# A hybrid mLSTM and gMLP layer: the first weight chunk multiplied pass by pass, and each mLSTM head's operands loaded beside the head before

## The chip, the cores and the metric

The kernel runs on one core of one Trainium2 chip. The metric is the device time of one execution in microseconds (us). The kernel before was run three times: 1581.03, 1575.95 and 1568.94 us, median 1575.95. One further execution was recorded by the hardware profiler.

## What is computed

The layer takes x (512 tokens of 2048 features, float32), and returns the same shape. Cut to what matters:

```python
xn = rmsnorm(x, norm_w)
q, k, v_m, o_m, z_m, i_pre, f_pre, u_g, v_g, z_g = split_cols(xn @ w_in)
q, k = silu(causal_depthwise_conv([q, k]))          # width 4
log_i, log_f = i_pre + b_i, log_sigmoid(f_pre + b_f)
# 8 mLSTM heads (q, k: 128 wide, v: 256), causal, chunks of 128 tokens:
#   S = (q @ k.T) * P,  P = exp of gate sums, row by row stabilised
#   h = (S @ v + state part) / max(|denominator|, exp(-m))
y_m = rmsnorm_per_head(h) * mlstm_norm_w * sigmoid(o_m) * silu(z_m)
# 8 gMLP groups: token mixing by a lower triangular 128 x 128 matrix
y_g = gelu(u_g) * (w_s @ layernorm(gelu(v_g)) + b_s) * silu(z_g)
out = rmsnorm(x + [y_m, y_g] @ w_out, final_norm_w)
```

## The kernel before, in words

Every float32 operand of a matmul is cut into a high and a low half of a shorter format (a cast on ScalarE, ACT; a subtraction on VectorE, DVE), and a product is the sum of three matmuls: high x high, high x low, low x high. So each operand costs a cast and a subtraction before TensorE (PE) can use it. Names end in h and l accordingly: xah and xal, wh and wl, qkh and qkl. In the first chunk the high and low halves of one quarter of x both carry the name a.

The program is written with a framework of tiles: pools with a few buffers each, and semaphores where one engine's instruction needs another's result. It decides the final order on each engine from the order in the code and from priorities, so the order is read from the compiled program. The stages are:

1. **The first unit** (lines 735 to 741). Eight chunks of weights, each 128 x 1024 floats (w_first), are multiplied by eight chunks of x in the plain way: 24 matmuls of 128 x 512 per chunk and 8 small gate products (L271). For each chunk the loop calls `load_x` and `load` (DMA, some chunks ahead), `split_x` (L197: the scaling by the norm's weight L205, casts L206, L207 and L210, subtractions L208, L209 and L211), `split` (L168 and L169) and `sums_x` (L215, further sums for later units). Ahead of the loop stand `split_x(0)`, `split(0)`, `gate_weights()`, `split_x(1)` and `split(1)`. The loads of x and of the first weights come in two halves.
2. **Units 1 to 27** (`products`, L769): the seven products of a Strassen scheme on the other columns of w_in, 42 matmuls of 128 x 256 per chunk, with DMA-accumulated weight sums (L150, L151), and conv, gelu, silu and layer norm beside them.
3. **The output projection of the gMLP half** (L803 to L831): four column quarters dq times eight groups g, 24 matmuls `og` of 128 x 512 each. Beside it runs the mLSTM. Its steps are closures in a queue `bg`, of which `run_bg(6)` takes six behind each chunk; a `pause` is an empty step.
4. **The output projection of the mLSTM half** (`q_m`), then the last groups (`fo`), the residual and the final norm.

The queue of stage 3 holds, in this order: `gates` (L286: gate sums, scans and exponentials, whose result c goes to DRAM as c_dram), six pauses, `gate_shifts` (transposes tps of the rows go), four pauses, `gate_columns` (transposes tps of gb and gr, copied to gst). Then for each head h, by `queue_head`:

- `st_load`: GpSimd (POOL) issues the loads of q and k (tiles qr), ACT casts (L530), DVE subtracts (qkl, L531).
- `st_load_v` and `st_cb`: loads and splits of v (tiles vr, L542 and L543), and the load of the row c of this head to all partitions (cb, L548).
- four `st_s`: the score products s in PSUM (L556 to L558), the weights P from cb (L563 to L567), their product p (DVE, L569) and its split (sh, sl, L581 and L582).
- two `turn` steps of the head before: transposes ytm of oz (L462), copied and stored for stage 4.
- four `st_sv`: the products nv (L595 to L597), copied to h and den by ACT (L598, L599).
- `st_norm`: the load of oz (L605), the denominator da (L609), its reciprocal rr, four squares jk on ACT (L616), sq, rn on POOL (L620), hc.
- `st_out`: oz scaled by h and hc (L628).

s, nv, ytm and the gate transposes share four PSUM banks (pm), taken in turn; the `og` sums hold the other four. A bank of s comes free when p (L569) has read it, one of ytm or nv when ACT has copied it.

Of the kernel before, what the change touches and what calls it, by code (L numbers as in the profile page):

```python
# [9 lines left out]
F32 = mybir.dt.float32  # L10
# [37 lines left out]
def hybrid_layer(ctx, tc, xs, x, w_first, w_mid, w_gate, w_out, w_last, par, bif, ws_t, sgu, fin_w, out):  # L48
# [17 lines left out]
    def temp(name, dt=F32):  # L66
        return tp.tile([P, S], dt, tag="t", name=name)
# [84 lines left out]

    def split(n):
# [5 lines left out]
        if kind == "std":  # L159
            if n >= NF0 + 2:  # L160
                h = xb.tile([P, 2, S], F32R, tag="xb", name=f"fh{n}")
                l = xb.tile([P, 2, S], F32R, tag="xb", name=f"fl{n}")
            else:
                h, l = (wp.tile([P, WS], F32R, tag=tag, name=f"{tag}{n}", bufs=bufs)[
                    :, OFF:OFF + 1024].rearrange("p (a b) -> p a b", a=2) for tag, bufs in (("wh", 3), ("wl", 3)))
            f = t[:, 0:1024].rearrange("p (a b) -> p a b", a=2)
            for a in ((slice(0, 1), slice(1, 2)) if n == 0 else (slice(0, 2),)):
                nc.scalar.copy(h[:, a, :], f[:, a, :])  # L168
                nc.vector.tensor_tensor(l[:, a, :], f[:, a, :], h[:, a, :].bitcast(F32), op=ALU.subtract)  # L169
            splits[n] = (h, l)  # L170
            return
# [25 lines left out]
    def split_x(j):  # L197
        if j >= NP:
            return
        (ra, rb) = xr[j]  # L200
        ah, al = (xa.tile([P, 3, H], F32R, tag="xa", name=f"xa{c}{j}") for c in "hl")
        a21 = temp(f"a21_{j}", F32R).rearrange("p (a b) -> p a b", a=2)
        for b, r in enumerate((ra, rb)):
            k = j + NP * b
            nc.vector.tensor_scalar(r, r, prm[:, C_NW + k:C_NW + k + 1], None, op0=ALU.mult)  # L205
        nc.scalar.copy(ah[:, 0, :], ra[:, 1, :])  # L206
        nc.scalar.copy(a21[:, 0, :], ra[:, 0, :])  # L207
        nc.vector.tensor_tensor(al[:, 0, :], ra[:, 1, :], ah[:, 0, :].bitcast(F32), op=ALU.subtract)  # L208
        nc.vector.tensor_tensor(a21[:, 1, :], ra[:, 0, :], a21[:, 0, :].bitcast(F32), op=ALU.subtract)  # L209
        nc.scalar.copy(ah[:, 1:3, :], rb)  # L210
        nc.vector.tensor_tensor(al[:, 1:3, :], rb, ah[:, 1:3, :].bitcast(F32), op=ALU.subtract)  # L211
        X[j] = [(ah[:, s, :], al[:, s, :]) for s in range(3)]
        A21[j] = (a21[:, 0, :], a21[:, 1, :])
# [416 lines left out]

    def queue_head(h):
        if h < NH:
            bg.append(lambda: st_load(h))
            bg.append(lambda: st_load_v(h))
            bg.append(lambda: st_cb(h))
            for s0 in range(NT):
                bg.append(lambda s0=s0: st_s(h, s0))
        if h > 0:
            for f in range(2):
                w = prm[:, C_MW + 2 * (h - 1) + f:C_MW + 2 * (h - 1) + f + 1]  # L640
                bg.append(lambda f=f, w=w: turn("m", h - 1, f, oz_t[h - 1], w))
            bg.append(mark(("m", h - 1)))
        if h < NH:
            for t0 in range(NT):
                bg.append(lambda t0=t0: st_sv(h, t0))
            bg.append(lambda: st_norm(h))
            bg.append(lambda: st_out(h))
# [60 lines left out]
    split_x(0)  # L708
    split(0)
# [6 lines left out]
    for j in range(NP):  # L716
# [16 lines left out]
        for q in range(4):  # L733
            cs = slice((q % 2) * P, (q % 2 + 1) * P)
            for kk in range(2):
                xh, xl = blocks[kk][q // 2]
                st, sp_ = (j == 0 and kk == 0), (j == NP - 1 and kk == 1)
# [51 lines left out]
    bg.append(gates)  # L789
    bg.extend([pause] * 6)  # L790
    bg.append(gate_shifts)
    bg.extend([pause] * 4)
    bg.append(gate_columns)
    for h in range(NH + 1):
        queue_head(h)

# [193 lines left out]
```

## Time and profile before

| | |
|---|---|
| runs | 1581.03, 1575.95, 1568.94 us; median 1575.95 |
| profiled execution | 1567.65 us |
| its span in the profile | 1565.6 us |
| mean granted TensorE clock | 0.995 |
| PE / PEld / DVE / ACT / POOL busy | 1531.3 / 1465.1 / 1181.9 / 876.7 / 285.6 us |
| first unit | 0 to 63 us; heads beside the output projection: about 1155 to 1350 us |

The span runs from the first instruction to the last; 2.05 us of the profiled execution lie outside it. PE is matmuls and PEld their weight loads, which overlap. In rows of time, the first number is the start from the span's beginning and the second the duration, both in us; `out<-in` are tiles. In brackets stands how long the engine had been idle before, and what ended that. Matmuls are pipelined, so that in a dense row of them one lasts longer than the time until the next starts.

### The profile page before, as it was taken

The numbers are of one execution on the slowest core, as the hardware profiler recorded it, in microseconds if no ns is written. First come the engines' busy times: TensorE is split into PE (matmuls) and PEld (weight loads), VectorE is DVE, ScalarE is ACT, GpSimd is POOL, SyncE is SP. The second block draws the span as 40 slices with busy tenths as digits, with TensorE's granted clock in tenths as the row PEclk, the third lists the DMA queues.
The fourth block names the chain that finished last, engine by engine and source line by source line (L and its number), as shares of the span: only waits on it lengthen the run. The fifth ranks groups of instructions, "written<-read, shape, count | busy, mean of one in ns | idle before, by whom it ended". The sixth has DMA issues, their size and how long they took to land.

```text
span 1565.6 us, 30099 instructions
## 1 busy us (share of the span) xinstructions
PE 1531.3 (98%) x11864; PEld 1465.1 (94%) x11864; DVE 1181.9 (75%) x1944; ACT 876.7 (56%) x1340; POOL 285.6 (18%) x384
## 2 busy tenths in 40 slices
PE   8999999999999999999999999999999999999997
PEld 7899999999999999999999999999977777889986
DVE  7877767877976877977877977779785565587875
ACT  5665555664654565554655556465676666453343
POOL 2321112211122211122211111111112222011100
PEclk9999999999999999999999999999999999999999
DMA  8777787787778787878787777878765565698972
GB/s 289 222 192 196 210 207 204 187 210 196 213 201 214 191 216 191 217 190 219 196 215 193 210 190 211 223 203 208 232 204 192 179 200 175 232 279 232 272 237 108
DMA packets 118509, 326.99 MB, mean 209 GB/s; under 512 B 13533, under 2 KB 20701, under 8 KB 118368
## 3 DMA queue, kind: packets, MB, share of 16 engines
q1 hardware_dynamic: 77456, 243.30, 48.2%
q0 software_dynamic: 40192, 80.66, 26.9%
q8 instruction: 93, 1.52, 0.4%
q10 hardware_dynamic: 720, 1.11, 0.2%
q14 instruction: 48, 0.39, 0.1%
HBM read 229.37 MB, written 32.74 MB: 167 GB/s over the span
## 4 chain that ended last, share of the span: by engine, by line
PE 67%; DVE 12%; DMA 8%; issue 6%; ACT 4%; POOL 1%; SPq 0%; ACTq 0%; POOLq 0%; DVEq 0%
PE q L769 56%; DVE wl L179 2%; DMA wf<-wf 2%; PE q_m L769 1%; DMA wf<-w_mid 1%; ACT wh L178 1%; PE og L822 1%; PE og L823 1%; PE og L821 1%; DMA xr<-xs 1%; ACT jk L616 1%; PE fo L886 1%; PE fo L887 1%; PE fo L885 1%; DMA ymd<-yfm 1%
## 5 line engine op out<-in xcount | busy, mean ns | idle before, releaser
L178 ACT CAST wh<-wf 128x1280 fp32r<-128x1280 f32 x240 | 301.8, 1263 | 356.0 <-issue 205.8
L179 DVE TENSOR_TENSOR wl<-wf,wh 128x1280 fp32r<-128x1280 f32 x240 | 356.2, 1486 | 152.8 <-ACT wh L178 152.7
L769 PE MATMUL q<-wh,xbh 128*128 128x256 f32 x1472 | 410.7, 279 | 1.4 <-ACT e L745 1.4
L769 PE MATMUL q<-wl,xbh 128*128 128x256 f32 x1472 | 410.2, 279 | 1.7 <-DVE wl L179 1.6
L769 PE MATMUL q<-wh,xbl 128*128 128x256 f32 x1472 | 409.6, 278 | 0.0
L151 POOL DMA_DIRECT2D wf<-wf x240 | 204.8, 855 | 997.8 <-DMA wf<-w_mid 259.6
L769 PE MATMUL q<-wh,xah 128*128 128x256 f32 x1104 | 309.6, 280 | 1.6 <-DVE e L362 1.3
L769 PE MATMUL q<-wl,xah 128*128 128x256 f32 x1104 | 307.3, 278 | 0.0
L769 PE MATMUL q<-wh,xal 128*128 128x256 f32 x1104 | 307.2, 278 | 0.0
L769 PEld LDWEIGHTS q<-wh,xbh 128*128 128x128 f32 x1472 | 278.3, 189 | 1.8 <-ACT e L745 1.6
L769 PEld LDWEIGHTS q<-wl,xbh 128*128 128x128 f32 x1472 | 277.0, 188 | 2.9 <-DVE wl L179 2.5
L769 PEld LDWEIGHTS q<-wh,xbl 128*128 128x128 f32 x1472 | 276.6, 188 | 0.0
L769 PEld LDWEIGHTS q<-wh,xah 128*128 128x128 f32 x1104 | 208.7, 189 | 2.1 <-DVE e L362 1.5
L769 PEld LDWEIGHTS q<-wl,xah 128*128 128x128 f32 x1104 | 207.8, 188 | 0.1
L769 PEld LDWEIGHTS q<-wh,xal 128*128 128x128 f32 x1104 | 207.4, 188 | 0.0
L178 ACT CAST wh<-we 128x512 fp32r<-128x512 f32 x240 | 147.8, 616 | 94.1 <-DVE we L176 93.6
L179 DVE TENSOR_TENSOR wl<-we,wh 128x512 fp32r<-128x512 f32 x240 | 164.3, 685 | 17.2 <-ACT wh L178 17.2
L175 DVE TENSOR_TENSOR we<-wf 128x256 f32<-128x256 f32 x240 | 101.1, 421 | 25.8 <-issue 14.8
L176 DVE TENSOR_TENSOR we<-we,wf 128x256 f32<-128x256 f32 x240 | 101.1, 421 | 5.4
L821 PE MATMUL og<-wh,ygh 128*128 128x512 f32 x256 | 100.6, 395 | 1.6 <-ACT wh L168 1.6
L822 PE MATMUL og<-wl,ygh 128*128 128x512 f32 x256 | 100.8, 394 | 0.1
L823 PE MATMUL og<-wh,ygl 128*128 128x512 f32 x256 | 100.4, 392 | 0.0
(272 smaller groups left out, 2858.1 us busy)
## 6 DMA issues: line engine op xcount, KB each, us to landing
wf<-w_mid SPq DMA_DIRECT2D x216, 640.0 KB, 4.9
wf<-wf POOLq DMA_DIRECT2D x240, 256.0 KB, 5.2
wf<-w_out_p SPq DMA_DIRECT2D x40, 512.0 KB, 4.0
wf<-w_last SPq DMA_DIRECT2D x24, 640.0 KB, 5.2
xr<-xs SPq DMA_DIRECT2D x16, 256.0 KB, 6.4
xt<-x SPq DMA_DIRECT2D x8, 512.0 KB, 7.5
ozd<-e SPq DMA_DIRECT2D x16, 256.0 KB, 3.0
ygd<-yfg SPq DMA_DIRECT2D x16, 256.0 KB, 4.6
```

The costliest lines, as they stand in the source:

```text
L151: nc.gpsimd.dma_start(t[:, 3 * H:5 * H], t[:, H:3 * H], accum_op=ALU.add)
L175: nc.vector.tensor_tensor(e[:, 0:H], t[:, 3 * H:4 * H], t[:, 2 * H:3 * H], op=ALU.add)
L176: nc.vector.tensor_tensor(e[:, H:2 * H], e[:, 0:H], t[:, 0:H], op=ALU.add)
L178: nc.scalar.copy(h[:, c], f)
L179: nc.vector.tensor_tensor(l[:, c], f, h[:, c].bitcast(F32), op=ALU.subtract)
L616: nc.scalar.activation(junk, ht[t0 // 2][:, t0 % 2, 0:H], AF.Square, scale=rr[:, t0:t0 + 1], accum_out=ssq[:, t0:t0 + 1])
L769: nc.tensor.matmul(o, lhsT=st_, rhs=mv_, start=(first and a == 0), stop=(last and a == 2), skip_group_check=True)
L821: nc.tensor.matmul(acc[q], lhsT=yh[:, kk, cs], rhs=wh[:, kk, :], start=st, stop=False)
L822: nc.tensor.matmul(acc[q], lhsT=yh[:, kk, cs], rhs=wl[:, kk, :], start=False, stop=False)
L823: nc.tensor.matmul(acc[q], lhsT=yl[:, kk, cs], rhs=wh[:, kk, :], start=False, stop=sp_)
L885: nc.tensor.matmul(ps, lhsT=yh[:, kk, cs], rhs=h[:, kk, :], start=st, stop=False)
L886: nc.tensor.matmul(ps, lhsT=yh[:, kk, cs], rhs=l[:, kk, :], start=False, stop=False)
```

## The change

It has two parts, independent of each other.

**The first chunk.** `split_x` can do its two halves one at a time, and a new `split_first(a)` splits one half of the first weights. They are called in turn: half 0 of x, half 0 of the weights, half 1 of x, half 1 of the weights. The 24 matmuls of the first chunk run pass by pass over the four sums q: for each half kk four times high x high, four times (x low) x (weight high), four times (x high) x (weight low). Before, all six products of one sum came before the next sum in the code.

**The heads.** `st_load(h + 1)` stands behind the four `st_s(h)`, and `st_load_v(h + 1)` and `st_cb(h + 1)` behind the four `st_sv(h)`. Head 0's three loads stand right behind `gates`. There are six pauses instead of four before `gate_columns`, and six new ones before the `turn` steps of the last head.

The diff:

```diff
+    def split_first(a):
+        if 0 not in splits:
+            splits[0] = tuple(wp.tile([P, WS], F32R, tag=tag, name=f"{tag}0", bufs=3)[:, OFF:OFF + 1024].rearrange(
+                "p (a b) -> p a b", a=2) for tag in ("wh", "wl"))
+        h, l = splits[0]
+        f = raws[0][:, a * S:(a + 1) * S]
+        nc.scalar.copy(h[:, a, :], f)
+        nc.vector.tensor_tensor(l[:, a, :], f, h[:, a, :].bitcast(F32), op=ALU.subtract)
...
-            for a in ((slice(0, 1), slice(1, 2)) if n == 0 else (slice(0, 2),)):
-                nc.scalar.copy(h[:, a, :], f[:, a, :])
-                nc.vector.tensor_tensor(l[:, a, :], f[:, a, :], h[:, a, :].bitcast(F32), op=ALU.subtract)
+            nc.scalar.copy(h, f)
+            nc.vector.tensor_tensor(l, f, h.bitcast(F32), op=ALU.subtract)
...
-    def split_x(j):
+    def split_x(j, parts=(0, 1)):
...
+        for b in parts:
+            r = xr[j][b]
             k = j + NP * b
             nc.vector.tensor_scalar(r, r, prm[:, C_NW + k:C_NW + k + 1], None, op0=ALU.mult)
...
+            if b == 0:
...
+                nc.scalar.copy(ah[:, 0, :], r[:, 1, :])
+                nc.scalar.copy(a21[:, 0, :], r[:, 0, :])
+                nc.vector.tensor_tensor(al[:, 0, :], r[:, 1, :], ah[:, 0, :].bitcast(F32), op=ALU.subtract)
+                nc.vector.tensor_tensor(a21[:, 1, :], r[:, 0, :], a21[:, 0, :].bitcast(F32), op=ALU.subtract)
+            else:
+                ah, al = X[j].pop()
+                nc.scalar.copy(ah[:, 1:3, :], r)
+                nc.vector.tensor_tensor(al[:, 1:3, :], r, ah[:, 1:3, :].bitcast(F32), op=ALU.subtract)
...
+    def queue_loads(h):
+        bg.append(lambda: st_load(h))
+        bg.append(lambda: st_load_v(h))
+        bg.append(lambda: st_cb(h))
+
     def queue_head(h):
...
+        for s0 in range(NT):
+            bg.append(lambda s0=s0: st_s(h, s0))
+        if h + 1 < NH:
+            bg.append(lambda: st_load(h + 1))
+        queue_turns(h - 1)
+        for t0 in range(NT):
+            bg.append(lambda t0=t0: st_sv(h, t0))
+        if h + 1 < NH:
+            bg.append(lambda: st_load_v(h + 1))
+            bg.append(lambda: st_cb(h + 1))
+        bg.append(lambda: st_norm(h))
+        bg.append(lambda: st_out(h))
...
-    split_x(0)
-    split(0)
+    split_x(0, (0,))
+    split_first(0)
+    split_x(0, (1,))
+    split_first(1)
     gate_weights()
...
-        for q in range(4):
+        if j == 0:
+            for kk in range(2):
+                for xp, w in ((0, wh), (1, wh), (0, wl)):
+                    for q in range(4):
+                        cs = slice((q % 2) * P, (q % 2 + 1) * P)
+                        nc.tensor.matmul(acc[q], lhsT=blocks[kk][q // 2][xp][:, cs], rhs=w[:, kk, :],
+                                         start=(kk == 0 and xp == 0 and w is wh), stop=False)
+        for q in range(4 if j else 0):
...
     bg.append(gates)
+    queue_loads(0)
     bg.extend([pause] * 6)
     bg.append(gate_shifts)
-    bg.extend([pause] * 4)
+    bg.extend([pause] * 6)
     bg.append(gate_columns)
-    for h in range(NH + 1):
+    for h in range(NH):
         queue_head(h)
+    bg.extend([pause] * 6)
+    queue_turns(NH - 1)
```

What it does to the order of the compiled program is seen at three places. First DVE at the start of the program; xr_172 is the first chunk's x (its two halves one after the other), xal, a_0 and wl the low halves of x and of the weights. Before:

```order
L205 TENSOR_SCALAR xr_172<-xr_172,prm 128x512
L208 TENSOR_TENSOR xal_186<-xr_172,xah_185 128x256
L205 TENSOR_SCALAR xr_172<-xr_172,prm 128x512
L209 TENSOR_TENSOR a_0_187<-xr_172,a_0_187 128x256
L169 TENSOR_TENSOR wl_197<-wf_174,wh_196 128x512 x2
L211 TENSOR_TENSOR xal_186<-xr_172,xah_185 128x512
```

And now:

```order
L211 TENSOR_SCALAR xr_172<-xr_172,prm 128x512
L219 TENSOR_TENSOR xal_187<-xr_172,xah_186 128x256
L220 TENSOR_TENSOR a_0_188<-xr_172,a_0_188 128x256
L211 TENSOR_SCALAR xr_172<-xr_172,prm 128x512
L160 TENSOR_TENSOR wl_194<-wf_174,wh_193 128x512 x2
L224 TENSOR_TENSOR xal_187<-xr_172,xah_186 128x512
```

The low half of a no longer stands behind the scaling of x's second half (the second row with xr); both low halves of the weights still do. On PE the matmuls of the first chunk now come in fours.

Second DVE between head 0 and head 1; qkl, vl and p are of head 1, da to oz of head 0. Before, the splits of q and k of head 1 stood behind oz of head 0:

```order
L609 SCALAR_TENSOR_TENSOR da_14189<-den_14111 128x4
L610 TENSOR_TENSOR da_14189<-da_14189,gst 128x4
L612 RECIPROCAL rr_14192<-da_14189 128x4
L618 TENSOR_SCALAR sq_14194<-sq_14194 128x4
L622 TENSOR_TENSOR hc_14203<-rr_14192,rn_14201 128x4
L628 SCALAR_TENSOR_TENSOR oz_0_14185<-h_0_14110,hc_14203,oz_0_14185 128x256 x2
L628 SCALAR_TENSOR_TENSOR oz_1_14187<-h_2_14127,hc_14203,oz_1_14187 128x256 x2
L531 TENSOR_TENSOR qkl_0_14212<-qr_0_14209,qkh_0_14211 128x512
L169 TENSOR_TENSOR wl_14338<-wf_14155,wh_14337 128x1024
L531 TENSOR_TENSOR qkl_1_14218<-qr_1_14215,qkh_1_14217 128x512
```

Now:

```order
L542 TENSOR_TENSOR qkl_0_14113<-qr_0_14110,qkh_0_14112 128x512
L542 TENSOR_TENSOR qkl_1_14119<-qr_1_14116,qkh_1_14118 128x512
L620 SCALAR_TENSOR_TENSOR da_14219<-den_14123 128x4
L621 TENSOR_TENSOR da_14219<-da_14219,gst 128x4
L623 RECIPROCAL rr_14222<-da_14219 128x4
L554 TENSOR_TENSOR vl_0_14200<-vr_0_14197,vh_0_14199 128x2x256
L574 SCALAR_TENSOR_TENSOR p_0_14273<-cb_14213,gst,mask 128x128
L554 TENSOR_TENSOR vl_1_14208<-vr_1_14205,vh_1_14207 128x2x256
L574 SCALAR_TENSOR_TENSOR p_1_14288<-cb_14213,gst,mask 128x128
L629 TENSOR_SCALAR sq_14224<-sq_14224 128x4
L574 SCALAR_TENSOR_TENSOR p_2_14301<-cb_14213,gst,mask 128x128
L633 TENSOR_TENSOR hc_14233<-rr_14222,rn_14231 128x4
```

The splits of q and k have moved ahead of da; the splits of v and the first step of p for head 1, which stood behind oz of head 0, stand between rr and hc.

Third PE between the score products s of head 1 and the transposes ytm of head 0. Before, eight og products lay between them, of which the first two and the last two are shown:

```order
L558 MATMUL s_3_14309<-qkh_0_14211,qkl_1_14218 128x256
L823 MATMUL og_1_13835<-wh_14157,ygl_13797 128x512
L821 MATMUL og_1_13835<-wh_14157,ygh_13796 128x512
...
L823 MATMUL og_2_13836<-wh_14157,ygl_13797 128x512
L821 MATMUL og_2_13836<-wh_14157,ygh_13796 128x512
L462 MATMUL ytm_0_14319<-ident,oz_0_14185 128x128 x2
```

Now 24 do, a whole chunk, of which the first two and the last two are shown:

```order
L569 MATMUL s_3_14309<-qkh_0_14112,qkl_1_14119 128x256
L853 MATMUL og_0_13834<-wh_14132,ygh_13796 128x512
L854 MATMUL og_0_13834<-wl_14133,ygh_13796 128x512
...
L854 MATMUL og_3_13837<-wl_14133,ygh_13796 128x512
L855 MATMUL og_3_13837<-wh_14132,ygl_13797 128x512
L473 MATMUL ytm_0_14361<-ident,oz_0_14215 128x128 x2
```

So a chunk of the output projection has come between s and ytm here. In heads 2 and 5 it stands between s_0 and s_1 instead, and in head 7 only two og products lie between s and ytm.

More of the change, by code (lines that the diff above doesn't have):

```diff
@@ L195, in load_x @@
                 load(0)
-    def split_x(j):
+    def split_x(j, parts=(0, 1)):
         if j >= NP:
             return
[L200 to L203, printed above, removed]
+        for b in parts:
+            r = xr[j][b]
             k = j + NP * b
             nc.vector.tensor_scalar(r, r, prm[:, C_NW + k:C_NW + k + 1], None, op0=ALU.mult)
[L206 to L213, printed above, removed]
+            if b == 0:
+                ah, al = (xa.tile([P, 3, H], F32R, tag="xa", name=f"xa{c}{j}") for c in "hl")
+                a21 = temp(f"a21_{j}", F32R).rearrange("p (a b) -> p a b", a=2)
+                X[j] = [(ah[:, s, :], al[:, s, :]) for s in range(3)] + [(ah, al)]
+                A21[j] = (a21[:, 0, :], a21[:, 1, :])
+                nc.scalar.copy(ah[:, 0, :], r[:, 1, :])
[6 more added lines that the diff above has]
+                nc.vector.tensor_tensor(al[:, 1:3, :], r, ah[:, 1:3, :].bitcast(F32), op=ALU.subtract)
     def sums_x(j):
@@ L629, in st_out, with queue_turns @@
                                            in1=d, op0=ALU.mult, op1=ALU.mult)
+    def queue_loads(h):
+        bg.append(lambda: st_load(h))
+        bg.append(lambda: st_load_v(h))
+        bg.append(lambda: st_cb(h))
     def queue_head(h):
[L632 to L647, printed above, removed]
+        for s0 in range(NT):
[10 more added lines that the diff above has]
+        bg.append(lambda: st_out(h))
+    def queue_turns(h):
+        if h < 0:
+            return
+        for f in range(2):
+            w = prm[:, C_MW + 2 * h + f:C_MW + 2 * h + f + 1]
+            bg.append(lambda f=f, w=w: turn("m", h, f, oz_t[h], w))
+        bg.append(mark(("m", h)))
     Y = {}
@@ L736, in hybrid_layer @@
                 xh, xl = blocks[kk][q // 2]
-                st, sp_ = (j == 0 and kk == 0), (j == NP - 1 and kk == 1)
+                st, sp_ = False, (j == NP - 1 and kk == 1)
                 nc.tensor.matmul(acc[q], lhsT=xh[:, cs], rhs=wh[:, kk, :], start=st, stop=False)
```

## The prediction

> **What bounds the kernel now.** I read the engines' totals first. TensorE (PE) is busy for nearly the whole span, the others are not:
>
> ```profile
> PE 1531.3 (98%) x11864; PEld 1465.1 (94%) x11864; DVE 1181.9 (75%) x1944; ACT 876.7 (56%) x1340; POOL 285.6 (18%) x384
> ```
>
> The change neither adds nor removes a matmul, so all that it can win is idle time of PE, and time in which PE's clock is halved. Busy time in three stretches tells where that lies: the columns are the stretch, its length, then busy time (and instructions) of PE, PEld, DVE, ACT and POOL, the granted clock, the DMA engines' busy share and GB/s.
>
> ```profile
> 6.67:20.00 13.33, 11.64 (x42) 9.27 (x43) 10.07 (x22) 6.57 (x14) 3.11 (x2) 0.74 0.84 317
> 80.00:1100.00 1020.00, 1018.29 (x8767) 1013.97 (x8765) 793.39 (x1210) 574.98 (x744) 193.67 (x225) 1.00 0.79 204
> 1150.00:1400.00 250.00, 235.43 (x1204) 194.38 (x1203) 163.06 (x343) 148.66 (x362) 45.34 (x101) 0.99 0.63 204
> ```
>
> The thousand microseconds in the middle are full. The start loses 13.33 - 11.64 = 1.7 us and runs at 0.74 of the clock; the stage of the output projection with the mLSTM heads beside it loses 250 - 235.43 = 14.6 us. What PE waited for (sum in us, times, longest):
>
> ```profile
> PE s L557 <- DVE qkl L531: 4.8, 7, 1.1
> PE ytm L462 <- DVE p L569: 3.9, 4, 1.8
> PE p L739 <- DVE wl L169: 1.7, 1, 1.7
> PE og L821 <- ACT wh L168: 1.6, 1, 1.6
> PE tps L349 <- ACT gb L317: 1.3, 1, 1.3
> PE q_m L769 <- DVE xr L826: 1.1, 1, 1.1
> PE s L558 <- DVE qkl L531: 0.7, 3, 0.4
> PE ytm L462 <- DVE oz L628: 0.6, 1, 0.6
> ```
>
> Without the p L739 row, which is the start's, these sum to 14.0 us, nearly all of the 14.6. The og row and the q_m row (2.7 us) lie outside the change. That leaves 5.5 us for the split of q and k, 3.9 for a PSUM bank that the score product p holds, 1.3 before the gate transposes and 0.6 for oz.
>
> **The first chunk.** Its start in order of time (start, duration, engine, line, operation, tiles; in brackets the idle time before and its releaser):
>
> ```profile
> 6.67 0.74 PE L738 MATMUL p<-wh,xah 128*128 128x512 f32 x2 [1.50 <-ACT wh L168]
> 7.25 0.62 PE L738 MATMUL p<-wh,a 128*128 128x512 f32 x2
> 8.08 0.49 DVE L205 TENSOR_SCALAR xr<-xr,prm 128x512 f32<-128x512 f32 x1 [1.83 <-DMA xr<-xs]
> 8.81 1.29 DVE L169 TENSOR_TENSOR wl<-wf,wh 128x512 fp32r<-128x512 f32 x2
> 9.55 0.80 PE L739 MATMUL p<-wl,xah 128*128 128x512 f32 x1 [1.69 <-DVE wl L169]
> 14.41 0.63 PE L740 MATMUL p<-wh,a 128*128 128x512 f32 x1
> 14.84 0.52 PE L738 MATMUL p<-wh,xah 128*128 128x512 f32 x1
> 15.66 0.40 PE L739 MATMUL p<-wl,a 128*128 128x512 f32 x1
> 15.90 0.39 PE L740 MATMUL p<-wh,a 128*128 128x512 f32 x1
> 17.06 1.05 ACT L168 CAST wh<-wf 128x1024 fp32r<-128x1024 f32 x1 [2.63 <-PE p L740]
> ```
>
> After four matmuls PE is out of operands: wl stands on DVE behind the scaling of x's second half, whose load lands at 8.08. After the change the next four products take the low half of x's first half, which DVE now makes ahead of that scaling. They last until 9.2 to 9.6 (four at 0.33 to 0.43 us), when the first half of wl (8.08 + 0.4 + 0.65 = 9.1) is done too. So the hole of 1.69 us closes. Its size at the chunk's end (17.06, where the cast that waits for it starts) depends on the clock: from start to start a matmul takes 0.43 us up to 14.84, and 0.24 later. If the full clock comes where it did, at about 15.1, then of the 20 matmuls and one of the next chunk from 7.87 on 7.2 / 0.43 = 17 go at 0.43 and 4 at 0.24: the end is 16.1, 1.0 earlier. But it came 5.5 us after PE had taken up work without a hole (9.55); now that is so from 6.67 on, so it may come at 12.2: then 10 go at 0.43 and 11 at 0.24, the end is 14.8, 2.3 earlier.
>
> How much reaches the end of the stage is set by DVE later on:
>
> ```profile
> 32.40 0.33 SPq L150 DMA_DIRECT2D wf<-w_mid  x1
> 47.44 0.43 DVE L175 TENSOR_TENSOR we<-wf 128x256 f32<-128x256 f32 x1 [3.21 <-DMA wf<-wf]
> 48.12 1.22 DVE L169 TENSOR_TENSOR wl<-wf,wh 128x1024 fp32r<-128x1024 f32 x1
> 50.50 0.40 PE L739 MATMUL p<-wl,xah 128*128 128x512 f32 x1
> ```
>
> And the stretch before it in the view by stretches, for DVE alone (length, DVE busy, granted clock, DMA share, GB/s):
>
> ```profile
> 32.00:48.00 16.00, 12.40 (x28) 1.00 0.99 342
> ```
>
> Chunk 6 needs its wl (done 49.34) at 50.50, so PE alone can gain 1.2 us there; beyond that, the load of the first mid weights (issued 32.40, when a buffer came free behind PE) must land before 47.44. The DMA engines are full from 32 to 48 (0.99) but had room before (0.84 up to 20, in the row further up), so an earlier issue helps in part. I take 1.5 us, between 0.5 (half of the 1.0, the rest lost in the waits behind 47.44) and 2.3.
>
> **q and k loaded beside the head before.** A head in the old order:
>
> ```profile
> 1180.36 0.28 PE L597 MATMUL nv<-vh,s 128*128 128x258 f32 x1
> 1185.88 1.67 DVE L628 SCALAR_TENSOR_TENSOR oz<-h,hc,oz 128x256 f32<-128x256 f32 x4
> 1187.47 0.68 DVE L531 TENSOR_TENSOR qkl<-qr,qkh 128x512 fp32r<-128x512 f32 x1
> ```
>
> The split qkl follows oz of the head before, and oz ends 7.2 us after that head's last nv matmul. In the new order qkl of head h+1 stands ahead of da and oz of head h, right behind the splits of s. Its load is issued after those too, but then come head h's nv products (1176.62 to 1180.36, 3.7 us, the first row stands below) and 14 to 24 og products of 0.24 us before the next s: 7 to 9.5 us of PE, where a load may take as long as the cb row at the end of this text (5.7 at worst) and a split 0.7. So I count the whole 5.5 us as gained.
>
> **The p bank and the clock.** The longest stall and what came with it:
>
> ```profile
> 1214.16 0.66 PE L462 MATMUL ytm<-ident,oz 128*128 128x128 f32 x4 [0.72 <-DVE p L569]
> 1216.89 1.12 PE L462 MATMUL ytm<-ident,oz 128*128 128x128 f32 x4 [1.83 <-DVE p L569]
> 1218.88 0.63 PE L823 MATMUL og<-wh,ygl 128*128 128x512 f32 x1
> ```
>
> The fifty microseconds around it, by stretches of all engines:
>
> ```profile
> 1200.00:1250.00 50.00, 45.98 (x234) 38.20 (x233) 27.75 (x62) 29.87 (x86) 10.20 (x24) 0.97 0.61 201
> ```
>
> Behind the two holes of 2.55 us in all, an og product lasts 0.63 us, as at the halved clock of the start, and not 0.39 to 0.40. The mean clock of 0.97 over 50 us makes that 0.03 x 50 = 1.5 us lost. In the new order 24 og products (24 x 0.24 = 5.8 us) lie between the s products and ytm in heads 1, 3, 4 and 6, so p has time and their waits go: 3.9 + 1.5 us. But heads 2, 5 and 7 keep short seams: from the last nv to ytm there lie 24 og and the s products (three each of 512, 384, 256 and 256 columns, 2.0 us at 0.24 for 512), 7.8 us, against 7.2 for oz and 0.7 (the row of qkl, of the same shape) for p behind it. With no slack left I put 0.7 us back at each, 2.0 in all (0.3 to 4, the upper end being the old 3.9). ytm of the last head is put off by six pauses, so the 0.6 for oz goes.
>
> [...]
>
> **Head 0 and the gates.** Rows of the old order:
>
> ```profile
> 1164.81 0.54 POOL L315 DMA_DIRECT2D c_dram<-gb  x1 [12.39 <-DVE go L337]
> 1170.33 0.41 PE L349 MATMUL tps<-ident,gb 8*128 8x8 f32 x4 [1.27 <-ACT gb L317]
> 1174.68 0.69 DVE L582 TENSOR_TENSOR sl<-p,sh 128x512 fp32r<-128x512 f32 x1 [0.15 <-ACT sh L581]
> 1176.62 0.28 PE L595 MATMUL nv<-vh,sh 128*128 128x258 f32 x1
> ```
>
> With q, k and v of head 0 ahead of the shifts, and two more pauses, s runs before the gate transposes and these come later: 1.3 us of waits go. But DVE does the splits between the scans, so c leaves some 1.4 us (two splits of 0.7) later than 1164.81, and with it everything up to sh (done at 1174.68, then near 1176), while nv now stands where PE, without 1.3 us of waits and with fewer og products ahead, is at about 1174.7. I put 1.3 us back there (0 to 3).
>
> **The sum.** Start 1.5, qkl 5.5, p 3.9, clock 1.5, oz 0.6, gates 1.3: 14.3 us. Back: 2.0 for short seams, 1.3 for head 0, and 1.2 for waits that I don't see (three of 0.4, the longest in the s L558 row). That leaves 9.8, say 10 us. The profiled execution took 1567.65, 8.3 under the runs' median of 1575.95 (1568.94 to 1581.03); 10 off it is 1557.6. Against the median, by which I forecast, it is **1566 us**, 0.6% less.
>
> **Rivals.** *More than the sum* (0.25): the start's gain goes through at 2.3, and neither the unseen 1.2 nor half of what I gave back at the seams and head 0 comes, so 10 + 0.8 + 1.2 + 1.6 = 14 us, 1562; with all given back gone it is 10 + 0.8 + 4.5 = 15.3, and the runs' spread carries it past 15.8 in over half of these cases. For it: all waits named have work to cover them. Against: DVE and POOL run in order, and a wait often moves. *The waits move* (0.20): ytm and nv wait for the same chain (nv, den, rr, jk, rn, oz, p) as before, since only the head's beginning came earlier; then p's 3.9 and 1.5 stay and qkl's gain is halved, 10 - 5.4 + 2.0 - 2.7 = 4 us: 1572. For it: oz still ends 7.2 us after nv. *Slower* (0.10): on DVE the low halves of v and the first step of p for head h+1 now stand ahead of sq, hc and oz of head h, and on POOL the loads of v and cb ahead of oz's load and rn. If they land late, the chain to oz is held for everybody. What speaks for it:
>
> ```profile
> ACT p L567 <- DMA cb<-c_dram: 15.6, 5, 4.9
> DMA to landing us min/median/max: 3.3/3.4/5.7
> ```
>
> cb has 3.4 us in the median, at worst 5.7, and ACT already waits for it. Seven seams, so 10 us are eaten up at 10 / 7 = 1.4 us of lateness each; at 2.3 us with a halved clock for 1.5 more at each it is 7 x 3.8 - 10 = 17 us slower, 1593. Against: sq has to wait for four jk squares on ACT anyhow, and hc for rn, up to 1185.88 in the old head, 5.5 us behind nv: that covers a landing of 3.4.
>
> **Chances.** My forecast 0.45, the other three as given. 1% (15.8 us) is about what a measurement of this kernel can tell from no change. Faster by over 1%: 0.15 of the first rival and 0.07 of the forecast by the runs' spread, 0.22; slower by over 1%: 0.06 of the last, whose lateness may be small too, and 0.02 of the others, 0.08; within 1%: 0.70. The range takes in the bounds of the terms (1566 - 5 to 1566 + 6) and the runs' own spread of some 6 us: 1556 to 1577.
>
> **What would show it.** PE's list of waits without s <- qkl; between 7.87 and 17 no hole and chunk 0's end at 14.8 to 16.1; wf's landing before 47.44; no half clock near 1217; ytm <- p below 2 us in heads 2, 5 and 7. Wrong would be: DVE idle before vl or the cb steps with PE waiting for oz behind it, or over 15 us of idle PE in the heads' stage.

## The result, and the profile after

The changed kernel takes 1562.48 us (median of 13 runs, 1556.05 to 1571.57), the kernel before 1572.57 (13 runs, 1564.81 to 1581.32). The ratio is 0.9937, with a 95% interval of 0.9912 to 0.9963: 9.9 us faster, between 5.8 and 13.8. The forecast was 10 us.

The recorded execution of the changed kernel has a span of 1569.9 us, more than the 1565.6 before. It was the longest of its 13 runs (1571.57), so the two spans can't be set against each other, and the gain has to be looked for stage by stage. PE's list of waits after:

```profile
PE ytm L473 <- DVE oz L639: 2.5, 1, 2.5
...
PE og L853 <- ACT wh L176: 1.6, 1, 1.6
...
PE ytm L473 <- DVE p L580: 1.3, 3, 0.6
...
PE nv L606 <- ACT yfm L478: 0.7, 1, 0.7
```

No s waits for qkl any more, no tps for gb, and the first chunk's wait for wl is gone. Three waits at the transposes and at nv remain or are new: 2.5, 1.3 and 0.7 us. The same stretches as before, in the columns used there:

```profile
6.67:20.00 13.33, 13.33 (x56) 10.97 (x57) 12.37 (x27) 8.35 (x18) 1.98 (x2) 1.00 1.00 368
...
300.00:600.00 300.00, 299.71 (x2543) 298.59 (x2541) 229.55 (x353) 173.10 (x224) 56.45 (x66) 1.00 0.77 200
...
1150.00:1200.00 50.00, 48.29 (x240) 39.48 (x240) 36.09 (x75) 33.97 (x63) 7.84 (x21) 0.97 0.60 196
1200.00:1250.00 50.00, 46.32 (x233) 38.53 (x232) 33.35 (x75) 32.98 (x94) 12.27 (x27) 0.97 0.60 195
1250.00:1300.00 50.00, 49.50 (x264) 42.23 (x264) 31.94 (x67) 31.43 (x84) 12.53 (x33) 1.00 0.66 218
1300.00:1350.00 50.00, 49.37 (x275) 42.97 (x274) 27.24 (x60) 31.24 (x92) 9.04 (x18) 1.00 0.55 189
```

Between 6.67 and 20 us PE has no idle time left. The clock of 1.00 in this row leaves something out: the trace's record of the clock begins only at 9.68 here, and the products before that still follow each other by 0.43 us, as at the halved clock. In the heads' stage PE still loses 3.7 us between 1200 and 1250, most of it (2.5) at one place, and little behind it. The clock is halved for a while in two rows (0.97 each), where before it was one.

The row of 300 to 600 holds the surprise. The kernel before did 2571 matmuls there, and this one 2543, in code that the change doesn't touch and with next to no idle time:

```profile
300.00:600.00 300.00, 299.81 (x2571) 298.58 (x2571) 232.93 (x358) 173.14 (x224) 56.60 (x66) 1.00 0.78 203
```

That row is of the kernel before. From start to start a 128x256 product takes 113.3 ns in some stretches and 117.8 in others, and the recorded execution after has more of the latter. So every kernel below was read by four lengths of its trace, beside its ratio: where the first product of unit 1 starts (the start), how long units 1 to 27 last from there to the first og product (the middle, which no edit touches), how long it is from the first og product to the first q_m product (the heads' stage), and from there to the last instruction (the end). The halved clock is how long the clock stood at one half within the heads' stage, by the trace's record of it; half of that is counted as lost, an estimate from the og products, which follow each other by 0.43 us there (from 1167.43 in the changed kernel) and by 0.23 at full clock.

| kernel | start | middle | heads' stage | end | halved clock | ratio to before, 95% interval |
|---|---|---|---|---|---|---|
| before | 63.7 | 1076.3 | 251.1 | 174.5 | 3.4 | |
| before, recorded again | 63.1 | 1086.6 | 250.7 | 178.9 | 3.4 | 0.998 (0.996 to 1.001) |
| first chunk alone | 60.7 | 1081.0 | 250.6 | 176.0 | 3.4 | 0.998 (0.995 to 1.001) |
| passes alone | 61.5 | 1081.1 | 249.5 | 177.8 | 0 | 1.000 (0.998 to 1.003) |
| splits in turn alone | 63.1 | 1082.3 | 251.7 | 174.3 | 3.4 | 1.000, one run |
| heads alone | 64.0 | 1082.5 | 241.6 | 173.9 | 6.8 | 0.9925 (0.990 to 0.995) |
| changed | 60.3 | 1092.6 | 242.0 | 175.0 | 6.8 | 0.9937 (0.991 to 0.996) |
| changed, recorded again | 61.9 | 1092.6 | 238.6 | 173.9 | 3.4 | 0.990 (0.987 to 0.993) |
| v and cb earlier | 61.1 | 1089.0 | 246.3 | 174.2 | 10.2 | 0.996, one run |
| head 0 late | 61.0 | 1087.6 | 238.2 | 176.3 | 0 | 0.991, one run |
| q and k behind nv | 59.7 | 1091.1 | 236.8 | 175.7 | 0 | 0.994, one run |
| q and k behind output | 61.6 | 1084.7 | 248.0 | 174.7 | 10.2 | 0.996, one run |
| 18 steps a head | 61.0 | 1080.4 | 233.4 | 183.9 | 0 | 0.9915 (0.989 to 0.994) |
| 18 steps to head 5 | 60.4 | 1075.0 | 240.4 | 179.6 | 3.4 | 0.9935 (0.991 to 0.996) |

All in us. A ratio beside "one run" is that run's time over the median of before on the same chip, and has no interval. The start and the heads' stage repeat within 1 to 2 us as they were before the change (63.1 to 64.0 for the four with the old order of the products, 249.5 to 251.7 for the five with the old heads), and within 2 to 3.5 us as they are now (59.7 to 61.9 for the nine with both edits of the first chunk, 238.6 to 242.0 for the three with the heads of the change). So one trace tells two kernels apart in these stages only where they differ by more than such a spread, and in the middle, where one kernel differed by 10 us, it tells nothing.

### The profile page after: what moved, and what is told of

It reads as the page before. It is cut to its first block, busy times and chain, and to the rows that moved or that the text cites. A ratio compares the mean times of both kernels' runs of the same rounds, so it can differ in the third digit from the quotient of the medians.

```text
span 1569.9 us, 30095 instructions
## 1 busy us (share of the span) xinstructions
PE 1545.9 (98%) x11864; PEld 1485.4 (95%) x11864; DVE 1183.7 (75%) x1944; ACT 874.6 (56%) x1340; POOL 285.3 (18%) x384
## 5 line engine op out<-in xcount | busy, mean ns | idle before, releaser
L187 DVE TENSOR_TENSOR wl<-wf,wh 128x1280 fp32r<-128x1280 f32 x240 | 356.7, 1488 | 174.3 <-ACT wh L186 174.0
```

The lines of the kernel that those rows point to most:

```text
L187: nc.vector.tensor_tensor(l[:, c], f, h[:, c].bitcast(F32), op=ALU.subtract)
```

## The experiments

**The parts apart.** First the first chunk's part alone, that is the changed kernel with the old `queue_head` and queue:

```diff
-    queue_loads(0)
...
-    for h in range(NH):
+    for h in range(NH + 1):
         queue_head(h)
-    bg.extend([pause] * 6)
-    queue_turns(NH - 1)
```

> The first-chunk part alone, the heads as before. Theory (the two parts add up): the first product of unit 1 starts at 60.3 us as in the changed kernel (63.7 before), the stage from the first og product to the first q_m product lasts 251 us as before (242 in the changed kernel), and the time falls by about 3.4 us, 0.2%. Rival (the gain at the start is lost later, in waits of unit 1): the start at 60.3, but the time as before. A time within 0.3% of before would not tell these two apart; the starts in the trace do.

The start came to 60.7, the heads' stage to 250.6, the ratio to 0.998 (0.995 to 1.001). The start moved as expected. Whether it is given back later can't be read off: the middle differs by more than that between two traces of one kernel, and the runs can't resolve 0.2%, as the expectation said. The heads' part alone is the reverse, the old first chunk with the new queue:

> The heads part alone, the first chunk as before. Theory: first product of unit 1 at 63.7 us, the stage from the first og to the first q_m product 242 us, time about 8 us less, 0.5%. Rival (the heads' stage gains only because the start shifts the phase of the DMA queues): 246 us or more, time 0.2% less or none.

Start 64.0, heads' stage 241.6, ratio 0.9925. The gain of this stage doesn't need the first part. In the traces each part acts on a stage of its own: the start gains 2.6 us (63.5 in the mean of the four traces with the old order of the products against 60.9 for the nine with both edits of the first chunk), the heads' stage 10.4 (250.7 in the mean of the five with the old heads against 240.3 for the changed kernel's two).

The kernel before once more, unchanged:

> The kernel before once more, unchanged, for its trace. Two traces so far show 128x256 products in two paces, 113 to 114 ns and 118 ns from start to start, unit by unit. Theory: the pace is a matter of the execution, not of the change; this trace has other units at 113 than the first trace of before (12 of 27), and its time between the first product of unit 1 and the first og product, 1076.3 us there, differs by several us. Rival: the pace belongs to the kernel's addresses or order; the same units at 113, and 1076 us within 1. Ratio to before 1.000 within 0.4%.

The middle was 1086.6 instead of 1076.3, and the row of 300 to 600 had 2550 products:

```profile
300.00:600.00 300.00, 298.65 (x2550) 297.34 (x2549) 230.40 (x354) 173.21 (x224) 56.59 (x66) 1.00 0.78 200
```

The pace is a matter of the execution here: one kernel, 10.3 us apart in code that is the same. Start and heads' stage agree within 0.6 us.

**Which edit of the first chunk.** The order of the products alone, in the kernel before:

```diff
-        for q in range(4):
+        if j == 0:
+            for kk in range(2):
+                for xp, w in ((0, wh), (1, wh), (0, wl)):
+                    for q in range(4):
...
+        for q in range(4 if j else 0):
```

> Of the first-chunk part only the pass by pass order of the 24 products; the halves of x and of the weights are split in the old order, in which the low half of the quarter a stands behind the scaling of the second half of x. Theory (the order of the products is what closes the hole): first product of the gates at 14 to 15 us (17.05 before, 13.89 changed), unit 1 at 60.5 to 61.5. Rival (the splitting in turn is needed, since the second pass needs the low half of a): a hole of 0.8 to 1.7 us stays before the seventh product, gates at 15.5 to 16.5, unit 1 at 62 to 63.

The start was 61.5, with a hole of 0.46 us:

```profile
7.70 0.62 PE L738 MATMUL p<-wh,xal 128*128 128x512 f32 x2
8.79 0.74 PE L738 MATMUL p<-wh,a 128*128 128x512 f32 x2 [0.46 <-DVE a L209]
```

The seventh product waits for a, which still stands behind the scaling of x's second half. So the passes do most of it (63.5 to 61.5), and the splitting in turn takes the last hole away. What this is worth at the start of unit 1 isn't resolved: 61.5 lies within the 59.7 to 61.9 of the kernels with both edits, and in this trace the clock isn't seen to fall behind the hole (the product at 9.39 lasts 0.50 us, where the one at 9.43 with the splits in turn alone lasts 0.63). The rival's bound of 0.8 us for that hole was not reached. By itself, the splitting in turn does little:

> Of the first-chunk part only the splitting in turn, the 24 products in the old order, the heads as before. Theory (the order of the products is what closes the hole): the fifth product still waits for wl, 1.0 to 1.7 us, first gate product at 16 to 17 us (17.05 before, 13.89 changed), unit 1 at 62.5 to 63.7. Rival (it is the splitting): no hole over 0.5 us, first gate product at 14 to 15.

```profile
8.83 0.80 PE L752 MATMUL p<-wl,xah 128*128 128x512 f32 x1 [0.99 <-DVE wl L160]
```

The fifth product waits for wl for 0.99 us instead of 1.69, and the start stays at 63.1.

**Which edit of the heads.** The loads of head 0 behind the gate steps again:

```diff
     bg.append(gates)
-    queue_loads(0)
...
     bg.append(gate_columns)
+    queue_loads(0)
```

> The changed kernel with the loads of head 0 where they were, behind the gate steps. Theory (loading head 0 early is what takes away the wait before the gate transposes): the wait tps <- gb of 1.3 us comes back, the stage from the first og to the first q_m product gets 1 to 2 us longer, 243 to 244. Rival (the two further pauses do that): no wait of tps, 242.

```profile
PE og L853 <- ACT wh L176: 1.6, 1, 1.6
PE tps L360 <- ACT gb L328: 1.3, 1, 1.3
PE ytm L473 <- DVE p L580: 1.1, 3, 0.4
PE ytm L473 <- DVE oz L639: 0.7, 1, 0.7
```

The wait before the transposes of gb came back with 1.3 us, as expected: head 0's early loads remove it. But the stage was 238.2, not longer, with the wait of ytm for oz at 0.7 here and a clock that never halved. A single edit worth 1 us is lost among what the clock and the seams (the places where the transposes of one head meet the score products of the next) do.

Then q and k of the next head behind the four nv steps, with v and cb:

```diff
-        if h + 1 < NH:
-            bg.append(lambda: st_load(h + 1))
         queue_turns(h - 1)
         for t0 in range(NT):
             bg.append(lambda t0=t0: st_sv(h, t0))
         if h + 1 < NH:
+            bg.append(lambda: st_load(h + 1))
             bg.append(lambda: st_load_v(h + 1))
```

> The changed kernel with q and k of head h+1 queued behind the four nv steps of head h, with v and cb, and not ahead of them. Theory (splitting q and k ahead of da and oz is what took the 5.5 us of s <- qkl away): waits of s for qkl come back at 2 us or more in sum, the stage at 241 to 245 us. Rival (the distance to the chunks did it, not the place of the load): no wait of s for qkl, stage 238 to 240.

The waits of s for qkl stayed at 0.2 us, the stage was 236.8. The expectation failed, and the rival's 238 to 240 was missed too; it was also badly put, for in the compiled order qkl had moved behind da but was still ahead of sq, hc and oz. So the step from behind nv to ahead of nv, which the change took, isn't needed, as far as one trace shows. The next kernel puts q and k behind norm and output, where they were before the change, and leaves v and cb ahead:

```diff
-        if h + 1 < NH:
-            bg.append(lambda: st_load(h + 1))
         queue_turns(h - 1)
...
         bg.append(lambda: st_out(h))
+        if h + 1 < NH:
+            bg.append(lambda: st_load(h + 1))
```

> The changed kernel with q and k of head h+1 queued where they were before the change, behind norm and output of head h; v and cb stay ahead of these. The compiled order has qkl between hc and oz and behind oz again. Theory (a split of q and k that stands behind the chain da, jk, rn, hc, oz is what PE waited for, and a later s also leaves p less time ahead of ytm): waits of s for qkl 2 to 6 us in sum, waits of ytm for p 2 us or more, the stage from the first og to the first q_m product 242 to 249 us. Rival (v and cb being early is what shortens the stage; the place of q and k matters little): waits of s for qkl under 1 us, stage 236 to 240.

```profile
PE s L567 <- ACT qkh L541: 8.7, 4, 5.4
```

8.7 us of waits of s, and a stage of 248.0, with 5.1 lost to the halved clock. What PE waited for was the cast qkh and not the subtraction, since POOL issued the loads late; at the longest wait it had stood still for 4.97 us, until the store of xr to acc_dram was done. The rows:

```profile
1210.28 1.06 POOL L539 DMA_DIRECT2D qr<-qkd  x2 [4.97 <-DMA acc_dram<-xr]
...
1215.17 0.62 ACT L541 CAST qkh<-qr 128x512 fp32r<-128x512 f32 x1 [2.80 <-DMA qr<-qkd]
...
1217.03 0.79 PE L567 MATMUL s<-qkh,qkh 128*128 128x512 f32 x1 [5.43 <-ACT qkh L541]
```

So the change's 5.5 us hang on q and k being queued ahead of the chain norm and output. That the subtraction behind oz on DVE is what makes the difference is not shown by this kernel, whose loads were late already. The waits of ytm for p, expected at 2 us or more, didn't return; why was not looked into.

**What is left at the seams.** The wait of 2.5 us for oz is at head 2 (2.0 there in the second trace, 2.9 with the heads alone). The rows around it, in the changed kernel:

```profile
1211.20 0.54 POOL L548 DMA_DIRECT2D vr<-vd  x1 [2.51 <-DVE s L593]
...
1218.32 0.62 ACT L553 CAST vh<-vr 128x512 fp32r<-128x512 f32 x1 [5.76 <-DMA vr<-vd]
1218.84 1.05 ACT L176 CAST wh<-wf 128x1024 fp32r<-128x1024 f32 x1
...
1219.79 0.36 ACT L609 COPY h<-nv 128x256 f32<-128x256 f32 x1
...
1226.64 1.67 DVE L639 SCALAR_TENSOR_TENSOR oz<-h,hc,oz 128x256 f32<-128x256 f32 x4
...
1227.17 1.66 PE L473 MATMUL ytm<-ident,oz 128*128 128x128 f32 x4 [2.51 <-DVE oz L639]
```

The second half of v of head 2 was issued at 1211.20 and its cast started at 1218.32, 7.1 us later, the longest landing of such a load. ACT stood at this cast for 5.76 us with the copy of the last h of head 1 queued behind it; that nv product had been issued by 1217.0 and was copied at 1219.79. So oz ended at 1228.3, 11.3 us after the last nv, and not 7.2. I tried to mend it by loading v and cb with q and k:

```diff
         if h + 1 < NH:
-            bg.append(lambda: st_load(h + 1))
+            queue_loads(h + 1)
...
-        if h + 1 < NH:
-            bg.append(lambda: st_load_v(h + 1))
-            bg.append(lambda: st_cb(h + 1))
```

> The changed kernel with v and cb of head h+1 queued right behind q and k of head h+1, ahead of the transposes and nv of head h. Theory (the 2.5 us wait of ytm for oz in head 2 comes from the load of v, issued late and landing 7 us later, which holds DVE ahead of oz): DVE's idle time for the cast of v falls from 2.4 us in head 2 to under 1, no wait of ytm for oz over 1 us, the stage 238 to 240 us. Rival (the loads take long because of the projection's own traffic, whenever they are issued): the wait stays, 241 to 243 us.

```profile
PE nv L606 <- ACT yfm L478: 6.2, 2, 3.6
PE og L850 <- ACT wh L176: 1.6, 1, 1.6
PE ytm L473 <- DVE p L580: 1.5, 3, 0.9
```

The wait for oz went, but nv now waits 6.2 us for the copy yfm of ytm, since the cast of v stands ahead of that on ACT. The stage was 246.3, with 5.1 lost to the halved clock. Neither theory had foreseen this: the cast that held up the copy of h in the changed kernel (5.76 us) held up another copy here (3.6 us of PE at one place).

Two more kernels give each head more room, first with two empty steps behind each head:

```diff
         bg.append(lambda: st_out(h))
+        bg.extend([pause] * 2)
```

> The changed kernel with two empty steps behind each head's last, so that a head takes 18 steps, three chunks of the projection, and each head meets the chunks at the same place: 24 og products between s_0 and ytm, and 24 more between nv and the next s. Theory (what PE still waits for there is the chain nv, rr, jk, rn, oz, p at the heads whose seam is short): the waits ytm <- oz and ytm <- p go nearly all, the stage from the first og to the first q_m product falls from 242 to 235 to 238 us, the time by 4 to 7 us below the changed kernel, ratio to before 0.989 to 0.991. Rival (the late loads of v and cb set the chain, whatever stands between): DVE still idles for the cast of v for 2 us per head, waits of ytm or nv stay at 3 us or more in sum, the stage at 240 or more.

```profile
PE q_m L799 <- ACT wh L186: 2.5, 1, 2.5
PE q_m L799 <- DVE wl L187: 1.0, 1, 1.0
...
PE ytm L473 <- DVE oz L639: 0.6, 1, 0.6
```

As the theory had it, all waits at the seams vanish but the last head's 0.6, the clock stays up, and the stage falls to 233.4, 5 us less than in the better trace of the changed kernel. But the time doesn't follow: 0.9915 (0.989 to 0.994) beside the changed kernel's 0.990 (0.987 to 0.993), measured on the same chip. What was gained in the stage is gone behind it: the end takes 183.9 us, 9 to 10 more than in the changed kernel's traces. The first q_m products wait 3.5 us for their weights, and near 1503 the clock is halved for 6.8 us (3.4 lost) behind a wait of fo for em of 3.2, which the changed kernel has too (2.1 and 2.7) with full clock behind it. One reading of the first is that the heads' later end pushes the sums over the mLSTM outputs into the time when these weights are split. To test that, the empty steps were left out behind the last two heads:

```diff
+        bg.extend([pause] * (2 if h < 6 else 0))
```

> As the kernel with 18 steps per head, but the two empty steps only behind heads 0 to 5, so that the heads end some 0.7 of a chunk earlier. Theory (the steps that come later push the sums over the mLSTM outputs into the first chunks of the next stage, where they held DVE and cost 4.3 us): the stage from the first og to the first q_m product 233 to 236 us, waits of the first q_m products under 2.5 us in sum instead of 3.5, time 2 to 4 us below the changed kernel, ratio to before 0.986 to 0.990. Rival (the first chunks of the next stage wait for their own weights, whatever the heads do): 3.5 us or more of q_m <- wh and wl again and a ratio as for 18 steps, 0.9915.

```profile
PE og L855 <- DVE wl L177: 4.4, 2, 3.0
PE ytm L473 <- DVE p L580: 1.4, 2, 0.7
```

The waits moved ahead of the stage's end, to the last og products (4.4 us for wl), and one of 3.6 us for xr stands among the first q_m products; the stage was 240.4, the ratio 0.9935 (0.991 to 0.996). Neither theory's numbers held. That the later end of the heads crowds the splits on DVE fits both traces, but was not isolated. No version was shown to be faster than the changed kernel; the intervals overlap, and four of them ran once.

Last, the changed kernel once more:

> The changed kernel once more, unchanged, beside the runs of the kernel before on this chip. Theory (the gain lies in two stages and the rest is the pace of the 128x256 products, which differs between executions): first product of unit 1 at 60 to 61 us, the stage from the first og to the first q_m product 242 us within 1.5, the time between them anything from 1076 to 1093 us; ratio 0.991 to 0.996. Rival (the pace of the middle belongs to the changed kernel): 1092 us again, and the ratio nearer to 1.

Start 61.9, heads' stage 238.6, ratio 0.990: start and stage fell outside what was expected, by 0.9 and by 1.9 us. And the middle was 1092.6 us again. That speaks for the rival, and against a pace by mere chance; yet the ratio was better than the first time, which the rival excludes. Of the other six kernels with both edits of the first chunk and new heads, four have 1085 to 1091 us there, and two 1075 and 1080, so the slower pace doesn't come with the change as such. This execution too was the longest of its set (1568.76 of 1555.53 to 1568.76). Since these recorded executions lie some 6 to 9 us above their medians, the usual run of the changed kernel most likely has a shorter middle. Why both recorded ones fell on the slower pace stays open.

## Why the prediction was right, point by point

**The sum.** 10 us were forecast and 9.9 measured (5.8 to 13.8; the second set makes 16, 11 to 21). By the traces, the start gave 2.6 and the heads' stage 10.4, 13 in all. That lies within the runs' intervals. One premise of the sum was wrong, though: that all there is to win is idle time of PE and time at the halved clock. The heads' stage in the first trace of each kernel, before and after:

```profile
1140.00:1391.00 251.00, 237.55 (x1184) 195.00 (x1183) 161.67 (x342) 154.19 (x370) 44.79 (x101) 0.99 0.63 205
...
1152.90:1394.90 242.00, 235.47 (x1185) 197.56 (x1183) 163.05 (x342) 151.66 (x370) 45.35 (x101) 0.99 0.66 212
```

It is 9.1 us shorter. The idle time of PE fell by 6.9 us (13.4 to 6.5), and the halved clock took 1.7 back, so 3.9 us were gained in time that counts as busy. Most of this lies in the s products, here one of the three kinds, before and after (count, busy time in us, mean ns of one, idle time before them):

```profile
L557 PE MATMUL s<-qkl,qkh 128*128 128x512 f32 x8 | 3.9, 486 | 4.8 <-DVE qkl L531 4.8
...
L568 PE MATMUL s<-qkl,qkh 128*128 128x512 f32 x8 | 3.1, 391 | 0.0
```

In the old order those of 512 columns mostly follow each other by 0.34 us, in the new one by 0.23, with no idle time shown between them. Without idle time and what the halved clock costs, all s products take 18.9 us before and 15.8 after, and the og products 179.2 and 177.6. This holds in every trace: the stage without both is 235.8 to 236.3 us in the five with the old heads and 231.3 to 232.8 in the nine with the new. In the kernel with q and k behind the output, where s waits again, 10 of the 24 products of 512 columns follow each other by 0.34 us again. So the list of waits understated what the old order cost; why these products are slower beside such waits was not looked into.

That the sum came out at 10 is in part luck. In the first trace, these 3.9 us, 1.9 more at the start than forecast, and the 1.3 for head 0 and 1.2 for unseen waits that didn't come stand against 2.5 more at the seams and 3.2 less from the clock. This turns the forecast's 9.8 into 12.4, near the 12.5 of this pair of traces (3.4 at the start, 9.1 in the heads' stage).

**The first chunk: 1.5 forecast, 2.6 found.** The hole closed by the steps that the prediction named. The rows after:

```profile
7.63 0.49 DVE L211 TENSOR_SCALAR xr<-xr,prm 128x512 f32<-128x512 f32 x1 [1.05 <-DMA xr<-xs]
...
8.53 1.05 PE L760 MATMUL p<-wh,xal 128*128 128x512 f32 x2
9.39 0.76 PE L760 MATMUL p<-wh,a 128*128 128x512 f32 x2
9.98 0.63 PE L760 MATMUL p<-wl,xah 128*128 128x512 f32 x2
...
13.66 0.40 PE L767 MATMUL p<-wh,xah 128*128 128x512 f32 x1
...
44.01 0.43 DVE L183 TENSOR_TENSOR we<-wf 128x256 f32<-128x256 f32 x1 [3.42 <-DMA wf<-wf]
```

The low-half products fill the time up to 9.98, and the chunk ends near 13.9, 3.2 us earlier, and not at 14.8 to 16.1. The mis-sized step is the time of the clock: two products take 1.05 us at 8.53 (0.43 from start to start and 0.62 for the last), and 0.63 at 9.98, so the clock is full from before 10 on, where the prediction had 12.2. The prediction had taken the clock to come up 5.5 us after PE took up work without a hole. The kernel before shows otherwise: its first four products follow each other by 0.23 to 0.34 us, and by the trace's record the clock was full from 4.87, fell at 8.28, in the hole, and came back at 15.11, 6.8 us later. In the changed kernel's first trace the products follow each other by 0.43 us from 7.25 to 9.39, and the record has full clock from 9.68.

The load that was to limit the rest did so: in all fourteen traces unit 1 starts 16.25 to 16.33 us behind the row of we that shows its landing. It landed 3.4 us earlier in this trace (44.01 against 47.44), and at 43.5 to 45.6 in the nine traces with both edits against 46.8 to 47.7 in the four with the old order. Of the 2.8 us by which the first chunk ends earlier in the mean of these, 2.6 reach unit 1, where the prediction counted on a part.

**q and k: 5.5 forecast, 5.5 of waits gone**, and 3.1 us more in the s products themselves (above), which the prediction didn't have. No wait of s for qkl is left. That the place of the loads matters held in the kernel that put them behind the output again (8.7 us of waits); the reason held in part: the load's issue and the cast were late there, and not the subtraction.

**The p bank: 3.9, less 2.0 for short seams.** The waits for p fell from 3.9 to 1.3 us. The short seams were named rightly (heads 2, 5 and 7) and undersized: with 2.5 for oz and 0.7 for yfm, 4.5 us remained where 2.0 were put (3.0 in the second trace), 0.9 of it at head 1, which had been counted safe. 18 steps a head, which lengthen the seams, took nearly all of it away.

**The clock: 1.5 forecast as a gain, none found.** The stretch near 1217 was counted as gone with its stall. In the changed kernel's traces 6.8 and 3.4 us are at half clock and with the heads alone 6.8, before 3.4 in four of five; half of this is lost, so the change lost 1.7 us more in two of three traces and won nothing in the third. In the first trace, one of the two followed the wait of og for wh of 1.62 us:

```profile
1165.55 1.19 PE L853 MATMUL og<-wh,ygh 128*128 128x512 f32 x4 [1.62 <-ACT wh L176]
```

The kernel before had the same wait, of the same 1.62 us, and full clock behind it:

```profile
1152.67 1.19 PE L821 MATMUL og<-wh,ygh 128*128 128x512 f32 x4 [1.62 <-ACT wh L168]
```

The two waits lie differently to the changes of the clock. In each of the two traces the changes between its first record and the end of the work come whole multiples of 3.41 us after one another: at 8.28, 15.11, 1216.60 and 1220.01 in the kernel before (2, 352 and 1 times), at 1166.80, 1170.21, 1228.24 and 1231.65 in the changed one (1, 17 and 1 times). The rows below are windows cut at such multiples. In the changed kernel one window holds the whole wait, and the next one is at half clock; in the kernel before the wait lies across two windows, 0.7 us in one and 0.9 in the other, and the clock stays at 1.00. First the changed kernel, then the one before; the second number is PE's busy time, the third from the end the clock:

```profile
1163.38:1166.79 3.41, 1.74 (x7) 0.80 (x5) 3.40 (x5) 3.39 (x5) 1.31 (x6) 1.00 0.54 130
1166.80:1170.20 3.40, 3.36 (x8) 2.69 (x9) 2.70 (x4) 2.51 (x3) 0.00 (x0) 0.50 0.88 321
...
1148.33:1151.74 3.41, 2.72 (x13) 1.91 (x11) 1.46 (x3) 3.40 (x7) 0.47 (x1) 1.00 0.43 145
1151.75:1155.16 3.41, 2.39 (x9) 1.70 (x10) 2.73 (x4) 3.38 (x4) 0.61 (x2) 1.00 0.87 254
```

**Gates and oz: 1.9 forecast, 1.9 found**; the wait of tps for gb and that of the last head for oz are gone. The 1.3 us that were to come back at head 0 didn't: no nv of head 0 waits.

**The rivals.** "More than the sum" lies nearer than the forecast to the second set of runs (16 us), not to the first. Its price went up to 15.3 us, below 15.8, so the spread of the runs would carry it past 15.8 in fewer than half of its cases, and not in over half. "The waits move" had the right place (the chain nv to oz to ytm) but not the size: 4.5 us of waits remained. "Slower" had its mechanism at one seam: a late v held up the chain to oz by some 4 us and cost 2.5 of PE. It was mainly ACT's cast that held the chain, and not DVE, and one seam in seven was hit, so the price of 1.4 us at each was never near. Loading v earlier shows how close this lies: the stage got 4 to 8 us longer.

## What to carry to other kernels

When a chain ends late, look at what is queued ahead of it on each engine: moving the next head's first splits ahead of this head's last ones removed 5.5 us of waits, and putting a cast of late data ahead of a copy that others wait for cost up to 3.6 us at one place. Once the waits of one stage are gone, look at the next stage's operands: 18 steps a head made the stage 5 us shorter and its end 9 us longer, 3.5 of them in waits of the next stage's first products. A list of waits is not the whole price: here 6.9 us of idle time came with 3.9 more in products that follow each other faster. Where runs spread by 1%, take the gain from the lengths of the stages that the edit touches, in two traces of each kernel, and not from whole spans.

## What the runs showed of the hardware that was not expected

The pace of the 128x256 products has two values, 113.3 and 117.8 ns from start to start, with next to no idle time in either. Two stretches of the kernel before, of 35 us each:

```profile
190.00:225.00 35.00, 35.00 (x311) 1.00 0.86 222
390.00:425.00 35.00, 35.00 (x299) 1.00 0.80 219
```

It holds for tens of microseconds at a time. Two traces of one kernel had middles of 1076.3 and 1086.6 us; over the fourteen traces they go from 1075.0 to 1092.6. That is more than the whole change was worth, and about the spread of the runs. What sets the pace was not found.

The clock was halved after a wait of 1.62 us in one trace and not in another (above), so a stall's cost can't be told from its length alone. Both traces, cut into windows of 3.41 us at the changes of the clock, from its first record to the last matmul, have two windows each at full clock with a halved one behind them: PE was idle for 1.91 and 2.27 us in those of the kernel before, and for 1.67 and 2.48 in those of the changed one. The other windows at full clock have at most 1.27 us of idle time in the kernel before and 1.44 in the changed one. Idle time of this kind was not the only thing to go with a halved clock: in the second trace of the changed kernel an og product of 512 columns lasts 0.39 us at 1180.84 and 0.63 from 1185.07 on, with the small gate transposes between them and no idle time shown. What sets the clock was not shown.
